# A gate by seven products of quarters, added up in PSUM banks, in a hybrid trunk on one core

## The chip, the core and the metric

The kernel runs on one core of a Trainium2 chip. A core has TensorE (PE; its weight loads are listed apart as PEld), VectorE (DVE), ScalarE (ACT), GpSimd (POOL) and SyncE (SP), which here only issues DMA transfers. Working memory is SBUF, 128 partitions wide; matmul sums are made in PSUM, whose banks hold 128 x 512 fp32 values. The metric is device time in microseconds (us) of one execution.

## The reference

One layer of a trunk on x of 512 x 1024 in fp32. A single projection of the normalised input feeds three branches; each branch's result is multiplied by a sigmoid gate of its own, the three are added, and a feed-forward block follows.

```python
u = rmsnorm(x, ln1_g)
proj = u @ w_in
q, k, v, pool_in, z, xbc, dt_raw, gate_pre = jnp.split(proj, split_idx, axis=-1)
y_a = dilated_attention_mixer(q, k, v, rel_bias) @ w_a     # three groups of six heads
y_b = pool_mixer(pool_in, pool_w, pool_scale) @ w_b
y_c = ssd_mixer(z, xbc, dt_raw, ...) @ w_c
gates = jax.nn.sigmoid(gate_pre + b_gate).reshape(b, s, N_BRANCH, D_MODEL)
merged = gates[:, :, 0] * y_a + gates[:, :, 1] * y_b + gates[:, :, 2] * y_c
x = x + merged @ w_o
x = x + conv_ffn(rmsnorm(x, ln2_g), ffn_w_up, ffn_conv_w, ffn_conv_b, ffn_w_down)
return rmsnorm(x, final_g)
```

The change touches three pieces of `u @ w_in`: the 1024 columns of the second gate (`gates[:, :, 1]`), v of attention groups 1 and 2 (384 columns each, "the pair"), and q and k of attention group 1 (384 columns each).

## The kernel before, in words

**Split products.** Every fp32 operand is split into a high and a low part, and a product is three matmuls: high by high, high by low, low by high (`mm3`, L229 to L237). The activations u (`uh`, `ul`, transposed, 8 tiles of 128 features x 512 tokens) are split once; weights are split job by job.

**Jobs.** A job is a slab of weights, at most 128 x 2048 values, and a `body` that multiplies with it. Its raw tile is loaded by SyncE's DMA queue (`fetch`, L183, two buffers `wraw`), ScalarE makes the high part in two halves (`cast`, L196, three buffers `whp`), VectorE makes the low part (`low`/`lows`, L216, two buffers `wlp`), and a job may have a `then`, which is run behind its low part. The main loop takes the jobs in order: ahead of the body of job n it issues the low part of job n+1, puts the cast of job n+2 in a list that is worked off at the `step()` behind the body's matmuls, and fetches job n+3. Side work (attention, the scan, the convolutions' ends) is kept in generators, and each `step()` advances them by one piece.

**Order.** TensorE, ScalarE, VectorE and GpSimd execute in the order in which the program emits (the `ORDERED` set near the end); only DMA issues on SyncE are placed by a scheduler. The order of jobs is written out in `program()`. Around the change it is: pool projection, v of group 0, q/k of group 0, pool output, the branch product with w_b (its result, kept in `MG`, is what the second gate multiplies), gate chunks 0 to 3, the pair, q/k of group 1, attention of group 1 started as side work, gate chunks 4 to 7, the twelve XBC chunks, the scan.

**The gate.** `gate_jobs(1, ...)` are plain jobs of 256 columns: a chunk of 128 features x 512 tokens is 8 x 3 matmuls of 512 columns in a bank named `pa`, then a sigmoid on ScalarE (L1226) and a product with `MG` on VectorE (L1228).

**Products of quarters.** The pair and q/k of group 1 are done already by seven products for eight (`sevens` and `qk_sevens`): the activations are cut into two halves of features by two halves of tokens, the weights into two halves of rows by two halves of columns; seven products of sums of quarters give the four quarters of the result. The products are named one to seven. Sums of activation quarters come from `sums_of` (four rounds of VectorE and ScalarE, put in the branch product's stage before). Sums of weight quarters are made on VectorE by `diff` (L341), one per step from the last one, and cast and split like a raw tile. Before, each product has a fresh bank (`pb` or `pq`, of four), is copied to SBUF by ScalarE (L370, L735) or read by VectorE with additions to the products that came before, and the quarters of the result are emitted from SBUF (L662 for the pair, L745 for q/k).

Tiles of 128 x 512 fp32 come from a pool of `NBIG` = 54 through `T(name)`; the weight quarters that aren't loaded as raw tiles lie in `ypool`.

Of the kernel before, what the change touches and what calls it, by code (L numbers as in the profile page):

```python
# [10 lines left out]
F32 = mybir.dt.float32  # L11
# [5 lines left out]
P = 128  # L17
# [65 lines left out]
def trunk(ctx: ExitStack, tc, out, x, rel_bias, ln1_g, w_in, b_gate, w_a, pool_w, pool_scale, w_b,  # L83
# [10 lines left out]
    rows = ctx.enter_context(tc.tile_pool(name="rows", bufs=1))  # L94
# [5 lines left out]
    ypool = ctx.enter_context(tc.tile_pool(name="ypool", bufs=2))  # L100
# [221 lines left out]
    def sums_of(f0, f1, ah, al, found):  # L322


        sa, sb = T("sa"), T("sb")
        dve.tensor_tensor(sa[:, LO], f0[:, HI], f1[:, HI], OP.add)
        dve.tensor_tensor(sa[:, HI], sa[:, LO], f0[:, LO], OP.subtract)
        dve.tensor_tensor(sb[:, LO], f0[:, LO], f0[:, HI], OP.subtract)
        dve.tensor_tensor(sb[:, HI], f1[:, LO], sa[:, HI], OP.subtract)
# [13 lines left out]

    def sevens(quarter, c, side, W, emit):

        r1, r2, r3, r5 = {}, {}, {}, {}

        def job(j, load, form, use):  # L350
            def body(ws):
                wh, wl = ws
                parts = side(j)
                for i in range(2):
                    ps = MM("pb")
                    o = slice(i * P, (i + 1) * P)
                    mm3(ps[:, :c], lambda k: wh[:, k, :], lambda k: wl[:, k, :],
                        lambda k: parts[k][0][:, o], lambda k: parts[k][1][:, o], range(4), flip=True)
                    use(i, ps[:, :c])
                step()  # L360
            new = Job([load] if load is not None else [], 4, c, body)
            new.form = form
            if load is None:
                new.load = lambda: None
            return new

        def keep(r, name):
            def use(i, ps):
                r[i] = T(name)[:, :c]
                act.copy(r[i], ps)  # L370
            return use

        def p5(i, ps):
            keep(r5, "r5")(i, ps)
            dve.tensor_tensor(r2[i], r2[i], ps, OP.add)

        def p6(i, ps):
            dve.tensor_tensor(r1[i], r1[i], ps, OP.add)
            emit(0, 1, i, r1[i], r2[i])

        def p7(i, ps):
            r3[i] = T("r3")[:, :c]
            dve.tensor_tensor(r3[i], r1[i], ps, OP.add)
            emit(1, 1, i, r3[i], r5[i])

        one = job("A11", quarter(0, 0), None, keep(r1, "r1"))
        two = job("A12", quarter(1, 0), None, lambda i, ps: emit(0, 0, i, r1[i], ps))
        three = job(4, None, lambda: W[1], keep(r2, "r2"))
        one.then = lambda: diff(one.raw, W[0], one.raw)
        three.then = lambda: diff(W[0], W[1], W[0])  # L390
        two.then = lambda: diff(W[1], W[1], one.raw)
        yield one
        yield three
        yield two
        yield job(1, None, lambda: one.raw, p5)
        yield job(2, None, lambda: W[1], p6)
        yield job(3, None, lambda: W[0], p7)
        yield job("A22", None, lambda: diff(two.raw, two.raw, W[1]),
                  lambda i, ps: emit(1, 0, i, r3[i], ps))
# [3 lines left out]
    def sums_of_u(p):  # L403

        f = []
        for k in (2 * p, 2 * p + 1):
            f.append(T("uf"))
            dve.tensor_tensor(f[-1], uh[:, k, :].bitcast(F32), ul[:, k, :].bitcast(F32), OP.add)
        yield
        yield from sums_of(*f, T("sah", F32R), T("sal", F32R),  # L410
                           lambda j, h, l: US.__setitem__((j, p), (h, l)))
# [32 lines left out]
    def grow(src):  # L444
        g = rows.tile([P, D], F32, name="grow", tag="grow")
        sp.dma_start(g, src.partition_broadcast(P))
        return g
# [11 lines left out]
    def norm_early(t, g):  # L459
# [4 lines left out]
        pool.tensor_tensor(xg, t, g[:, :S], OP.mult)  # L464
# [3 lines left out]
    def norm_late(t, g, v0, outs, last=None):  # L468
# [6 lines left out]
        dve.tensor_tensor(xg, t, g[:, S:], OP.mult)  # L475
# [171 lines left out]
    def v_pair():  # L647

        c, W = C_V + 384, []
        vd = dram.tile([S, 384], F32, name="vdram")  # L650
        rows_ = lambda c0: w_in[:, c0:c0 + 384].rearrange("(k two p) c -> two p k c", two=2, p=P)
        quarter = lambda two, h: rows_(c + 384 * h)[two]

        def load():
            for two in range(2):
                W.append(ypool.tile([P, 4, S], F32, name="w3", tag="xs")[:, :, :384])
                sp.dma_start(W[two], quarter(two, 1))

        def emit(hi, right, i, a, ps):
            g, tb = 1 + right, 2 * hi + i  # L660
            t = T(f"v{g}")
            dve.tensor_tensor(t[:, :384], a, ps, OP.add)  # L662
            if g == 2:
                sp.dma_start(vd[tb * P:(tb + 1) * P, :], t[:, :384])
                return

            for n in range(4):
                if (g, n) not in V:
                    V[g, n] = T(f"vr{g}")
                sp.dma_start(V[g, n][32 * tb:32 * tb + 32, :384], t[n:P:4, :384])  # L670
# [8 lines left out]
        return load, sevens(quarter, 384, side_u, W, emit), residues  # L679
# [20 lines left out]
    def qk_sevens(g):  # L700


        W = []
# [3 lines left out]
        r1, r2, r3, r5 = {}, {}, {}, {}  # L707

        def load():
            for two in range(2):  # L710
                W.append(ypool.tile([P, 4, S], F32, name="w3", tag="xs")[:, :, :384])
                sp.dma_start(W[two], quarter(two, 1))

# [1072 lines left out]
```

## Time and profile before

| | us |
|---|---|
| runs (3) | 1023.88 to 1024.09, median 1024.09 |
| profiled execution | 1024.13 |
| its span | 1022.4 |
| TensorE busy | 1013.1 (99%), 5258 matmuls |
| TensorE weight loads | 857.6 (84%) |
| VectorE busy | 701.4 (69%), 890 instructions |
| ScalarE busy | 507.9 (50%), 847 instructions |
| GpSimd busy | 127.2 (12%), 108 instructions |
| DMA | 118.08 MB, 115 GB/s on average |

The span is the time from the first to the last recorded instruction; the execution's own time has 1.7 us more around it. A line such as `L216 DVE TENSOR_TENSOR wl<-raw,wh 128x2048 ... | 192.5, 2438 | 39.1 <-ACT wh L196` reads: line 216 of the kernel, VectorE, the output and inputs by name, the shape, then the group's busy time in us, the mean of one instruction in ns, and the time that the engine sat idle before these instructions with what ended it. Rows of the timeline begin with the start in us and the duration in us. Rows that begin with a stretch in us (180.50:204.61) give the busy time and the count of instructions of each engine in that stretch, then the clock that was granted to TensorE, the DMA engines' share and GB/s.

### The profile page before, as it was taken

The page shows a single profiled execution, that of the slowest core. Times are in us where ns is not written, and L with a number is a line of the kernel's source. Part 1 is how long each engine was busy: PE and PEld are TensorE (multiplying, and loading weights), DVE is VectorE, ACT ScalarE, POOL GpSimd, SP SyncE. Part 2 cuts the span into 40 slices and gives each one's busy share as a digit, 9 for nine tenths or more (in the row PEclk, how much of TensorE's full clock was granted, in tenths as well). Part 3 has the DMA queues.
Part 4 walks back from the last instruction along what each step waited for, and adds up shares of the span by engine and source line. Part 5 has one row for each costly group of instructions (what it writes and reads, how often), then busy time and mean ns, then how long its engine had stood idle before and what let it go on. Part 6 is the DMA issues. An engine that isn't in the chain of part 4 may idle for free.

```text
span 1022.4 us, 13249 instructions
## 1 busy us (share of the span) xinstructions
PE 1013.1 (99%) x5258; PEld 857.6 (84%) x5258; DVE 701.4 (69%) x890; ACT 507.9 (50%) x847; POOL 127.2 (12%) x108
## 2 busy tenths in 40 slices
PE   8999999999999999999999999999999999999997
PEld 8998878899888888888888888898888888888886
DVE  6563566788766656676879666768778768685756
ACT  5432545454574366878567224554444434433434
POOL 1770000000000000000044501102111100111002
PEclk9999999999999999999999999999999999999999
DMA  8444312124442354552254526542232333321322
GB/s 269 138 118 135 105 62 76 31 83 145 124 118 83 87 151 112 145 138 74 79 140 160 165 83 237 178 142 86 94 113 83 99 107 122 126 83 42 124 83 82
DMA packets 114077, 118.08 MB, mean 115 GB/s; under 512 B 6212, under 2 KB 97927, under 8 KB 114016
## 3 DMA queue, kind: packets, MB, share of 16 engines
q1 hardware_dynamic: 113423, 116.39, 37.0%
q8 instruction: 41, 0.67, 0.3%
q10 hardware_dynamic: 592, 0.86, 0.3%
q14 instruction: 21, 0.16, 0.1%
HBM read 113.44 MB, written 3.00 MB: 114 GB/s over the span
## 4 chain that ended last, share of the span: by engine, by line
PE 98%; DMA 1%; DVE 0%; ACT 0%; ACTq 0%; issue 0%
PE pa L237 36%; PE pu L237 22%; PE pb L237 12%; PE pd L237 7%; PE pqk L237 6%; PE pq L237 3%; PE pa L1633 2%; PE ps L799 1%; PE pu L1434 1%; PE ppw L237 1%; PE po L847 1%; PE pt L833 1%; PE py L1132 1%; DMA xin<-in_x_dram 1%; PE pyo L1139 1%; PE pst L1120 0%
## 5 line engine op out<-in xcount | busy, mean ns | idle before, releaser
L216 DVE TENSOR_TENSOR wl<-raw,wh 128x2048 fp32r<-128x2048 f32 (+3 forms) x95 | 220.1, 2318 | 47.5 <-ACT wh L196 39.7
L196 ACT CAST wh<-raw 128x1024 fp32r<-128x1024 f32 (+4 forms) x187 | 186.5, 1017 | 42.7 <-DVE raw L341 18.0
L1329 DVE SCALAR_TENSOR_TENSOR hc<-pu,fcol,hc 128x510 f32<-128x510 f32 x88 | 65.9, 748 | 56.4 <-ACT hc L1326 54.8
L237 PE MATMUL pa<-uh,wh 128*128 128x512 f32 x384 | 97.0, 395 | 0.0
L237 PE MATMUL pa<-ul,wh 128*128 128x512 f32 x384 | 94.9, 389 | 0.0
L237 PE MATMUL pa<-uh,wl 128*128 128x512 f32 x384 | 94.8, 389 | 0.0
L237 PEld LDWEIGHTS pa<-ul,wh 128*128 128x128 f32 x384 | 72.1, 188 | 15.1
L237 PEld LDWEIGHTS pa<-uh,wl 128*128 128x128 f32 x384 | 72.1, 188 | 14.9
L237 PE MATMUL pu<-uh,wh 128*128 128x512 f32 (+1 forms) x352 | 83.5, 379 | 0.0
L237 PE MATMUL pu<-uh,wl 128*128 128x512 f32 (+1 forms) x352 | 83.5, 379 | 0.0
L237 PE MATMUL pu<-ul,wh 128*128 128x512 f32 (+1 forms) x352 | 83.5, 379 | 0.0
L237 PEld LDWEIGHTS pa<-uh,wh 128*128 128x128 f32 x384 | 70.6, 188 | 14.3
L237 PEld LDWEIGHTS pu<-uh,wl 128*128 128x128 f32 x352 | 64.2, 188 | 12.5
L237 PEld LDWEIGHTS pu<-ul,wh 128*128 128x128 f32 x352 | 64.2, 188 | 12.4
L237 PEld LDWEIGHTS pu<-uh,wh 128*128 128x128 f32 x352 | 64.1, 188 | 12.4
L1326 ACT ACTIVATE hc<-pu,fcol,fcol 128x512 f32<-128x512 f32 x40 | 31.2, 779 | 78.9 <-PE pu L237 78.9
L1334 POOL TENSOR_TENSOR hc<-hc 128x512 f32<-128x512 f32 x22 | 30.8, 1401 | 289.0 <-DVE hc L1329 252.0
L1115 POOL TENSOR_TENSOR st<-st,dts 128x512 f32<-128x512 f32 x4 | 4.5, 1126 | 380.4 <-ACT st L1123 322.0
L821 ACT ACTIVATE sb<-sb,nmls 128x128 f32<-128x128 f32 (+1 forms) x72 | 30.0, 418 | 25.7 <-DVE nmls L818 13.6
L1331 ACT ACTIVATE hc<-hc 128x512 f32<-128x512 f32 x22 | 13.9, 632 | 39.9 <-DVE hc L1329 39.9
L1226 ACT ACTIVATE sg<-pa,col 128x512 f32<-128x512 f32 x24 | 16.5, 689 | 32.1 <-PE pa L237 31.0
L969 DVE SCALAR_TENSOR_TENSOR xs<-pa,col,xs 128x509 f32<-128x509 f32 (+2 forms) x24 | 18.0, 749 | 17.1 <-ACT xs L965 16.6
(393 smaller groups left out, 1872.6 us busy)
## 6 DMA issues: line engine op xcount, KB each, us to landing
raw<-in_w_in_dram SPq DMA_DIRECT2D x25, 1024.0 KB, 5.2
raw<-in_ffn_w_up_dram SPq DMA_DIRECT2D x22, 1024.0 KB, 5.1
raw<-in_w_o_dram SPq DMA_DIRECT2D x8, 1024.0 KB
raw<-in_ffn_w_down_dram SPq DMA_DIRECT2D x8, 1024.0 KB, 5.1
raw<-in_w_in_dram SPq DMA_DIRECT2D x14, 512.0 KB, 4.8
raw<-in_w_in_dram SPq DMA_DIRECT2D x6, 768.0 KB, 4.6
raw<-in_w_b_dram SPq DMA_DIRECT2D x4, 1024.0 KB, 5.1
al<-ad SPq DMA_DIRECT2D x16, 256.0 KB, 7.3
```

The source lines that it names most:

```text
L196: (other.tensor_copy if other and i else act.copy)(job.high[:, :, o], job.raw[:, :, o])
L216: (eng or dve).tensor_tensor(l[:, :, o], job.raw[:, :, o], h[:, :, o].bitcast(F32), OP.subtract)
L237: pe.matmul(ps, l, r, start=first and n == 0, stop=last and n == total - 1, skip_group_check=onto)
L799: pe.matmul(pss[i][:, o:o + w * P], q[r, n * P:(n + 1) * P], k[r, kb * P:(kb + w) * P], start=True, stop=True)
L821: act.activation(sb[:, off:off + w * P], sb[:, off:off + w * P], AF.Exp, bias=nm[:, n, h:h + 1], accum_out=ls[:, n, h:h + 1])
L969: dve.scalar_tensor_tensor(t[:, sh:], ps[:, :S - sh], col[:, o_cw + 12 * k + m:o_cw + 12 * k + m + 1], t[:, sh:], OP.mult, OP.add)
L1226: act.activation(s, ps, AF.Sigmoid, bias=col[:, o:o + 1])
L1326: act.activation(t, ps, AF.Identity, bias=ff["c1"][:, ff["b"] + m:ff["b"] + m + 1], scale=fw(2, m))
L1329: dve.scalar_tensor_tensor(t[:, sh:], ps[:, :S - sh], fw(k, m), t[:, sh:], OP.mult, OP.add)
L1331: act.activation(t, t, AF.Silu)
L1334: pool.tensor_tensor(a, a, t, OP.mult)
L1633: pe.matmul(first[2 * n + j][:, lo:hi], a[:, k, j * P:(j + 1) * P], b[:, k, lo:hi], start=a is wh and b is uh and k == 0, stop=a is wl and ...
```

## The change

The second gate is now also done by seven products of quarters, and all three groups (gate, pair, q/k) share one class, `Seven`. A group uses two pairs of PSUM banks, A and B. Product two has B to itself and its result is kept in SBUF (`keep`, ScalarE); five opens B and is kept; three adds onto five in the bank and is kept. One opens A; six, seven and four add onto it, one behind the other, and after one, six and seven VectorE adds the bank's sum to a kept product or takes it off (`done`; in place, for q/k straight into their tiles), which makes a quarter of the result; after four the bank holds the last quarter. For the gate ScalarE then takes sigmoids of 128 x 256 pieces (four per product), and the product with `MG` follows a step later (`total(m)`), when a 128 x 512 chunk is whole.

Of the sums of weight quarters one in four is made by four DMA transfers on GpSimd's queue that add a quarter from DRAM onto a loaded tile (`plus`); the other three stay on VectorE (`total`). The groups interlock: the next group's two comes ahead of the last group's four. The sums of activations are spread over two stages and made with other signs (`turned`); attention of group 1 is called behind the gate, pair and q/k groups and one XBC job. `ypool` has three buffers, `NBIG` is 52, and the row of gains is loaded as two T tiles in place of one tile of a pool of its own.

By the emitted order, TensorE has 5402 matmuls for 5258: 192 of 512 columns are replaced by 336 of 256. The pair and q/k keep theirs.

```diff
-    rows = ctx.enter_context(tc.tile_pool(name="rows", bufs=1))
...
-    ypool = ctx.enter_context(tc.tile_pool(name="ypool", bufs=2))
+    ypool = ctx.enter_context(tc.tile_pool(name="ypool", bufs=3))
...
-    def sums_of(f0, f1, ah, al, found):
...
+        plus, minus = (OP.subtract, OP.add) if turned else (OP.add, OP.subtract)
         sa, sb = T("sa"), T("sb")
-        dve.tensor_tensor(sa[:, LO], f0[:, HI], f1[:, HI], OP.add)
...
+    class Seven:
+        def __init__(self, quarter, c, widths, product, done, name):
+            R, A, B, W = {}, [], [], [None, None]
+            def tile_of(i):
+                W[i] = ypool.tile([P, 4, S], F32, name="w3", tag="xs")[:, :, :c]
+                sp.dma_start(W[i], quarter(i, 1))
+            def plus():
+                for k in range(4):
+                    pool.dma_start(W[0][:, k, :], quarter(0, 0)[:, k, :], accum_op=OP.add)
+            def total(out, a, b, op=OP.add):
+                dve.tensor_tensor(out, a, b, op)
+                return out
+            def job(j, raw, form, bank, use, more=False):
+                def body(ws):
+                    if not more:
+                        bank[:] = [MM(name) for _ in range(2)]
+                    for i in range(2):
+                        product(bank[i], ws, side_u(j), i, more)
+                        use(i, bank[i][:, :widths[i]])
+                    step()
+                new = Job([raw] if raw is not None else [], 4, c, body)
+                new.form = form
+                if raw is None:
+                    new.load = lambda: None
+                return new
+            def keep(hi, right):
+                def use(i, ps):
+                    r = R[hi, right, i] = T("r7")[:, :widths[i]]
+                    act.copy(r, ps)
+                return use
+            def end(hi, right, op=None):
+                return lambda i, ps: done(hi, right, i, R.get((hi, right, i)), ps, op)
+            self.two = job("A12", quarter(1, 0), None, B, keep(0, 0))
+            five = job(1, None, lambda: W[0], B, keep(1, 1))
+            three = job(4, None, lambda: W[1], B, keep(0, 1), True)
+            one = job("A11", quarter(0, 0), None, A, end(0, 0, OP.add))
+            six = job(2, None, lambda: W[0], A, end(0, 1, OP.subtract), True)
+            seven = job(3, None, lambda: W[1], A, end(1, 1, OP.subtract), True)
+            four = self.four = job("A22", quarter(1, 0), lambda: total(four.raw, four.raw, W[0]), A,
+                                   end(1, 0), True)
+            five.then = lambda: total(W[0], W[0], W[1])
+            one.then = lambda: total(W[1], W[0], one.raw, OP.subtract)
+            self.jobs = five, three, one, six, seven
+            self.load = lambda: tile_of(0), plus, lambda: tile_of(1)
...
+        def product(ps, ws, parts, i, more):
+            o = slice(i * P, (i + 1) * P)
+            mm3(ps[:, :384], lambda k: ws[0][:, k, :], lambda k: ws[1][:, k, :],
+                lambda k: parts[k][0][:, o], lambda k: parts[k][1][:, o], range(4), flip=True, onto=more)
+        def done(hi, right, i, r, ps, op):
             g, tb = 1 + right, 2 * hi + i
-            t = T(f"v{g}")
-            dve.tensor_tensor(t[:, :384], a, ps, OP.add)
+            if r is None:
+                r = T(f"v{g}")[:, :384]
+                act.copy(r, ps)
+            else:
+                dve.tensor_tensor(r, r, ps, op)
...
+    def by_features(chunks):
+        def product(ps, ws, parts, i, more):
+            for n, m in enumerate(chunks[i]):
+                o = slice(m * P, (m + 1) * P)
+                mm3(ps[:, 256 * n:256 * n + 256], lambda k: ws[0][:, k, o], lambda k: ws[1][:, k, o],
+                    lambda k: parts[k][0], lambda k: parts[k][1], range(4), onto=more or n > 0)
+        return product
...
+        def done(hi, right, i, r, ps, op):
+            which = "qk"[right]
...
+                view = (plain if right else grouped)(QK[which, g, m], g)[:, :, 64 * hi:64 * hi + 64]
...
+                if r is None:
+                    dve.tensor_copy(view, piece(ps))
+                else:
+                    dve.tensor_tensor(view, piece(r), piece(ps), op)
...
+    def gate_seven(b):
+        quarter = lambda two, h: w_in[:, C_GATE + b * D + S * h:C_GATE + b * D + S * h + S].rearrange(
+            "(k two p) c -> two p k c", two=2, p=P)[two]
+        chunks = ((0, 1), (2, 3))
+        def total(m):
+            dve.tensor_tensor(MG[m], MG[m], SG[b, m], OP.mult)
             return
...
+        def done(hi, right, i, r, ps, op):
+            if r is not None:
+                dve.tensor_tensor(r, r, ps, op)
+            for n, m in enumerate(chunks[i]):
+                m += 4 * right
+                if (b, m) not in SG:
+                    SG[b, m] = T("sg")
+                o = o_bg + 8 * b + m
+                act.activation(SG[b, m][:, 256 * hi:256 * hi + 256],
+                               (ps if r is None else r)[:, 256 * n:256 * n + 256],
+                               AF.Sigmoid, bias=col[:, o:o + 1])
+                if hi:
+                    running.append(after(1, total(m)))
+        return Seven(quarter, S, (512, 512), by_features(chunks), done, "pa")
...
         yield from v_jobs(0)
+        yield Call(lambda: running.extend(after(3 * p, sums_of_u(p)) for p in (0, 1)))
         yield from qk_jobs(0)
         yield from pool_out_job()
         yield Call(lambda: attend(0))
         yield Call(lambda: waiting.insert(3, ssd_prep()))
+        gates = gate_seven(1)
+        pair, residues_of_v = v_pair()
+        groups = gates, pair, qk_sevens(1)
         for i, job in enumerate(branch_jobs(1, w_b, YB, 8, more=range(7))):
-            if i == 3:
-                yield Call(lambda: running.extend(after(p, sums_of_u(p)) for p in range(4)))
+            if i == 1:
+                yield Call(gates.load[0])
+            if i == 2:
+                yield Call(lambda: running.extend(after(2 * p - 4, sums_of_u(p)) for p in (2, 3)))
+                yield Call(gates.load[1])
+                yield Call(gates.load[2])
             yield job
-        load, pair, residues_of_v = v_pair()
-        yield Call(load)
-        yield from gate_jobs(1, 0, SPLIT)
-        loads, qk = qk_sevens(1)
-        for i, job in enumerate(pair):
-            yield job
-            if i == 4:
-                yield Call(loads)
-        yield from qk
+        last = None
+        for group, next_ in zip(groups, groups[1:] + (None,)):
+            yield group.two
+            if last:
+                yield last.four
+            last = group
+            for i, job in enumerate(group.jobs):
+                if next_ and i >= 2:
+                    yield Call(next_.load[i - 2])
+                yield job
+        xbc = jobs_a(w_in, C_XBC, 12, uhk, ulk, KD, xbc_evac)
+        yield next(xbc)
+        yield last.four
         yield Call(lambda: attend(1))
         yield Call(lambda: running.extend(after(2, f()) for f in (residues_of_v, residues_of_bias)))
-        yield from gate_jobs(1, SPLIT)
-        yield from jobs_a(w_in, C_XBC, 12, uhk, ulk, KD, xbc_evac)
+        yield from xbc
...
-NBIG = 54
+NBIG = 52
```

More of the change, by code (lines that the diff above doesn't have):

```diff
@@ L342, in diff @@
         return out
[L344 to L399, printed above, removed]
@@ L474, in norm_late @@
         xg = T("xg")
-        dve.tensor_tensor(xg, t, g[:, S:], OP.mult)
+        dve.tensor_tensor(xg, t, g[1], OP.mult)
         if last:
```

84 lines of the change are left out of this document (15 added, 69 removed).

## The prediction

> **What bounds the kernel.** I read the page's slices and chain first, then the chain of waits on TensorE, then the busy times by stage.
>
> ```profile
> span 1022.4 us, 13249 instructions
> PE   8999999999999999999999999999999999999997
> DVE  6563566788766656676879666768778768685756
> PEclk9999999999999999999999999999999999999999
> PE 98%; DMA 1%; DVE 0%; ACT 0%; ACTq 0%; issue 0%
> ```
> ```profile
> PE uT L1650 <- DVE diag L1662: 1.4, 2, 0.8
> PE pa L1592 <- DVE ones L1583: 1.1, 1, 1.1
> ```
> ```profile
> 180.50:204.61 24.11, 24.11 (x131) 19.86 (x130) 16.80 (x25) 11.09 (x18) 0.00 (x0) 1.00 0.11 33
> 204.61:233.76 29.15, 29.15 (x170) 29.14 (x168) 24.38 (x25) 13.39 (x21) 0.00 (x0) 1.00 0.38 115
> 233.76:263.99 30.23, 30.23 (x254) 30.23 (x254) 26.25 (x28) 13.62 (x20) 0.00 (x0) 1.00 0.34 110
> 263.99:293.00 29.01, 29.01 (x155) 23.68 (x154) 17.71 (x23) 22.78 (x42) 0.00 (x0) 1.00 0.44 133
> ```
> TensorE is the whole chain, and its only waits lie in the first 10 us. The last rows are the changed stretch: gate chunks 0 to 3, the pair, the q/k sevens, then gate chunks 4 to 7 (columns: sum, PE, PEld, DVE, ACT, POOL, clock). TensorE is busy throughout at full clock, so the time here is TensorE's work plus any wait that the change creates. VectorE is the next engine: 24.38 of 29.15 and 26.25 of 30.23 us where products of quarters run now, 16.80 of 24.11 where the gate runs. The profiled execution took 1024.13 us, its span and 1.7 around it; the median of the runs is 1024.09, so the sum needs no shift.
>
> **TensorE's work.**
> ```profile
> 328.58 1.98 PE L237 MATMUL pa<-uh,wh 128*128 128x512 f32 x8
> 330.40 1.98 PE L237 MATMUL pa<-ul,wh 128*128 128x512 f32 x8
> ```
> ```profile
> 240.94 0.64 PE L237 MATMUL pq<-sbh,wh 128*128 128x256 f32 x4
> 241.43 0.64 PE L237 MATMUL pq<-sbl,wh 128*128 128x256 f32 x4
> ```
> Starts give the pitch: 8 of 512 columns in 1.82 us, 0.227 each. The q/k stage has 7 x 36 = 252 matmuls of 256 columns in 30.23 us, 0.120 each (0.49 per 4 in the last rows). The gate had 8 chunks x 24 = 192 matmuls of 512 columns, 43.5 us; it gets 7 products x 48 = 336 of 256 columns, 40.3 us. Gain: 3.2 us. An eighth of 43.5 would be 5.4; the half-width shape gives 2.2 of it back, since in the q/k stage the weight loads are as busy as the matmuls (30.23 of 30.23). The pair (168 matmuls in 29.15 us, 0.1735 each, 4.16 per product) and q/k (4.32 per product) keep their counts and shapes.
>
> **What the banks cost.** Before, every product took a fresh bank of four. Now one, six, seven and four add onto the same two banks, and each product's sum must be read out before the next may write. So product i+1 waits for: VectorE's read of bank 0 after product i, and its own low half (wl). VectorE and ScalarE go in program order: within a product VectorE does the next product's low, then the reads of two banks; ScalarE does four sigmoids, then the cast of the product after next. These durations go in:
>
> ```profile
> 268.07 2.28 DVE L216 TENSOR_TENSOR wl<-raw,wh 128x2048 fp32r<-128x2048 f32 x1
> ```
> ```profile
> 237.10 1.75 DVE L216 TENSOR_TENSOR wl<-w,wh 128x1536 fp32r<-128x1536 f32 x1
> 238.77 1.75 DVE L341 TENSOR_TENSOR w<-w,w 128x1536 f32<-128x1536 f32 x1
> ```
> ```profile
> 265.32 2.00 ACT L196 CAST wh<-raw 128x1024 fp32r<-128x1024 f32 x2 [5.24 <-DMA raw<-in_w_in_dram]
> ```
> ```profile
> 238.53 1.57 ACT L196 CAST wh<-raw 128x768 fp32r<-128x768 f32 x2
> 241.15 0.59 ACT L735 COPY rq<-pq 128x512 f32<-128x512 f32 x1 [1.04 <-PE pq L237]
> ```
> ```profile
> L341 DVE TENSOR_TENSOR raw<-w,raw 128x2048 f32<-128x2048 f32 x2 | 4.6, 2280 | 0.0
> L1484 DVE TENSOR_TENSOR x<-x,pb 128x512 f32<-128x512 f32 x8 | 5.4, 684 | 2.1 <-PE pb L237 2.1
> L1226 ACT ACTIVATE sg<-pa,col 128x512 f32<-128x512 f32 x24 | 16.5, 689 | 32.1 <-PE pa L237 31.0
> L821 ACT ACTIVATE sb<-sb,nmls 128x256 f32<-128x256 f32 x18 | 9.1, 504 | 19.2 <-DVE nmls L810 12.0 <-DVE nmls L818 7.1
> ```
> ```profile
> 204.61 0.87 PE L237 MATMUL pb<-wh,uh 128*128 128x384 f32 x4
> 204.81 0.69 ACT L1226 ACTIVATE sg<-pa,col 128x512 f32<-128x512 f32 x1 [2.98 <-PE pa L237]
> 205.54 0.69 DVE L1228 TENSOR_TENSOR yo<-yo,sg 128x512 f32<-128x512 f32 x1 [2.25 <-ACT sg L1226]
> ```
> A bank's reader starts 0.2 us after its last matmul (204.61 to 204.81); ScalarE to VectorE takes 0.04. A sigmoid of 256 columns has no row: between the 128x256 exponential's 0.504 and zero its pitch, back to back, I take as 0.42 (the 512 sigmoid's 0.689 less the 0.3 by which a 256 one is shorter); the ends of 0.35 and 0.50 move each step's four by 0.3 either way.
>
> With t from the start of the gate's product one:
> - A product's cast is issued behind the readers of the product two before it: ScalarE copies three's second bank (0.2 to 0.8), then casts six by 2.7; VectorE has low six at 5.05, reads one's first bank by 5.66. Six may start at 5.76: no wait.
> - One's second bank is done at 5.76, read by 6.65; sigmoids to 7.5; cast seven to 9.5; low seven to 11.8; only then VectorE reads six's first bank, to 12.43. Seven starts at 12.5 where 11.52 was due: 1.0 lost.
> - Six's second bank is read by 13.0; sigmoids to 14.1; cast of the pair's first product to 15.65, its low to 17.4; four's combination (2.28) to 19.6; VectorE reads seven's two banks to 20.8; sigmoids to 21.8; cast four to 22.85 (first half) and 23.8; low four to 26.1. TensorE is through seven at 18.3 and the pair's first product at 22.4, waits 0.4 for the first half, does 8 of four's 48 matmuls, and waits 2.3 for the low half. 2.75 lost.
>
> Against 27.2 of plain work four ends near 31: a loss of 3.7, all because low four sits behind ScalarE's sigmoids. The same working for the pair: low six comes at 4.5 (a 1.57 cast, a 1.75 low, the reads) where the product takes 4.16: 0.35. For q/k six waits for two reads of 0.6 behind its low, 4.99 against 4.32: 0.65. Bounds of these three together: 1.0 at least (only seven's wait, if the second stretch overlaps one handover more), 7 at most (below).
>
> **What is moved or free.** The bank restarts after waits: a pipeline break costs 0.1 (1.98 for eight against 1.82), twice or three times, 0.2. The remaining edits lie beside other work:
> - Gate chunks 4 to 7 lay beside attention of group 1; their sigmoids alternated with its exponentials, and each change reloads ScalarE's table:
>
> ```profile
> L1226 ACT ACT_TABLE_LOAD x10 | 12.8, 1283 | 0.2
> ```
> Six such loads fall away. TensorE never waited for them, so they are worth zero; uncovered each would be 1.28. Attention then lies beside ten XBC chunks where it had 4 gate and 12 XBC chunks; ScalarE was busy 22.78 of 29.01 us there with sigmoids and loads that are now gone, so it still ends under the chunks.
> - The gate's multiplication by its branch (8 of 0.69) is queued on VectorE behind low four and ahead of the pair's low one; counted in the lows that follow, still inside 4.16 of slack per product.
> - One of four combinations becomes four adding transfers on GpSimd's queue, in three groups. No row shows such a transfer; the nearest are GpSimd's last row ahead of the gate and two loads:
>
> ```profile
> 72.18 0.22 POOL L925 TENSOR_TENSOR psw<-psw,ramp 128x16 f32<-128x16 f32 x1
> ```
> ```profile
> raw<-in_w_in_dram SPq DMA_DIRECT2D x14, 512.0 KB, 4.8
> raw<-in_w_in_dram SPq DMA_DIRECT2D x6, 768.0 KB, 4.6
> ```
> The gate's and the pair's first quarters are now loaded at the head of SyncE's queue (three buffers), so both groups can be added from 72.4 on, as soon as GpSimd is through with that row; five's low wants them near 175. Only the third group waits, for the buffer that the gate gives up at four's combination, and q/k's five comes some 30 us later or more. At twice a load's time, 10 us for each, nothing is late; they cost zero while they take under 25 us, and at 35 the third would cost up to 10. GpSimd does nothing else in all four windows, so nothing is queued behind them that TensorE wants.
> - Behind SyncE's issues stand the raw loads, whose order is the old one; the DMA share is 0.11 to 0.44 in the four windows, so a raw tile keeps its 4.6 to 5 us and has a product's 5.76 after its buffer is free (two buffers: one is loaded while the other is cast). q/k and the pair had this in products of 4.2.
> - The opening moves 0.75 MB more (two tiles of 1.0 MB and one of 0.75 for two of 0.75 and a row of gains of 0.5). In the two rows by fortieth parts of the first 45 us (the DMA's share in tenths, then GB/s) that is 2.1 us at 350 GB/s, of a queue that then has a gap:
>
> ```profile
> DMA  0389999999999712489999999994000005990000
> GB/s 0 38 237 370 293 374 318 293 327 347 357 382 390 202 26 69 38 261 375 386 409 384 332 370 363 349 350 144 1 0 0 0 0 60 333 329 6 0 0 0
> ```
> ```profile
> 32.21 1.91 ACT L196 CAST wh<-raw 128x2048 fp32r<-128x2048 f32 x1
> ```
> The share falls to zero at some 31 us, and the cast that would feel the shift starts at 32.21. Zero, 1 us at the most.
> - Sums of the activations (four steps on VectorE and ScalarE) go in two pairs, one of them into the first q/k stage, where the slices of VectorE show 5 to 7 tenths. Zero, or 0.5 if a low slips behind them.
> - Two T tiles fewer (52), the gains' row loaded in two halves ahead of its use instead of at the start: zero, unless a tile is short.
>
> **The sum.** -3.2 + 3.7 + 0.35 + 0.65 + 0.2 = +1.7: 1025.8 us. From the bounds: -3.2 + 1.0 = -2.2 (1021.9), and -3.2 + 7 + 0.5 = +4.3 (1028.4). Of these the value stands nearest the middle because each of its starts is taken from a row, and only the sigmoid's pitch is not.
>
> **Rivals.**
> (1) The waits are hidden. If the reads and sigmoids come 1 us earlier each, by ScalarE taking cast seven ahead of one's last sigmoids or by finer waits on a tile's halves, only four's wait is left. The break-even is a loss of 3.2. For it: VectorE has 5 us spare per 29 now. Against: program order on ScalarE and the working above, which leaves no room. With a loss of 1.0: 1021.9. This ends on the other side.
> (2) More waits than counted. Here waits are held until a whole tile is written (a cast's second half, 23.8 for 22.85, adds 0.95 to four and as much to seven), and the pair's group takes the shift on, each product of it with 0.35. That is 2 x 0.95 + 4 x 0.35 = 3.3 more: 1029.
> (3) A late adding transfer: one group 5 us late gives 1030.8. The rows for loads speak against it.
> (4) The clock falls after a wait. The profile shows full clock everywhere with waits of at most 1.1 us; a wait of 2.3 is outside what it shows. The product behind four's wait (40 matmuls, 4.8 us) would run longer, by nothing at the least and by twice at the most: in the middle +2.4, 1028.2. The Trainium skill, "TensorE: Matmul & The Clock Gate", section "What's actually happening", says that the clock halves after an idle window of some 3.4 us, and returns after as much work; by that rule the wait here would be too short. If it did bite, its estimate is half of 3.4 us lost, 1.7.
>
> **Chances.** The forecast's case 0.50 (its own range 1024.5 to 1027.3), 1 0.22, 2 0.18, 3 0.05, 4 0.05. A measurement of this kernel tells 0.2% (2.05 us) from no change: under 1022.04 is faster, above 1026.14 slower. Faster holds most of rival 1: 0.17. Within 0.2% the rest of it and half of the forecast's case: 0.35. Slower: the other half, 2, 3 and 4, 0.48. The range goes from 1021.6 (rival 1) to 1029.5 (rival 2), leaving out late transfers and the deeper gains.
>
> **What would show it.** Waits of TensorE, none before in this stretch: on VectorE's read of six (pa) for 1.0 and on low four (wl) for 2 to 2.5; smaller ones in pb and pq. Gate matmuls of 256 columns at 0.120. The adding transfers all ended 15 us ahead of their products. Wrong it is if TensorE shows no wait on wl in gate four (rival 1), or waits on the tile that the adding transfer writes (rival 3), or a clock below 1.00 (rival 4).

## The result

The changed kernel takes 1029.3 us (median of 6, 1028.06 to 1029.51) where the kernel before takes 1024.0 (median of 6): a ratio of 1.0048, 95% interval 1.0035 to 1.0061. It is slower by 5.3 us, near the top of the range and 3.5 us above the point forecast. In a later batch the same kernel gave 1029.34 (median of 5, 1027.92 to 1030.68) beside 1024.05. Its executions fall into two groups: 4 of 11 lie at 1027.9 to 1028.3, 7 at 1029.2 to 1030.7. The profiled execution took 1028.16 us, span 1025.6, and belongs to the lower group.

From the page after the change, the span, the busy times and the chain:

```profile
span 1025.6 us, 13613 instructions
...
PE 1010.9 (99%) x5402; PEld 861.3 (84%) x5402; DVE 707.7 (69%) x886; ACT 511.2 (50%) x863; POOL 136.7 (13%) x120
...
PE 95%; DVE 2%; ACT 2%; DMA 1%; issue 0%; ACTq 0%
```

TensorE is busy for 1010.9 us where it was 1013.1, and yet the span is 3.2 us longer: VectorE and ScalarE now have 2% each of the chain, where they had none. TensorE's waits say where:

```profile
PE uT L1641 <- DVE diag L1653: 2.1, 2, 1.6
PE pa L236 <- DVE wl L215: 2.1, 1, 2.1
PE pa L1583 <- DVE ones L1574: 1.1, 1, 1.1
PE po L827 <- ACT sb L814: 0.8, 1, 0.8
PE pa L236 <- DVE r L741: 0.7, 1, 0.7
PE pq L236 <- DVE q L725: 0.6, 1, 0.6
PE pb L236 <- ACT wh L195: 0.2, 1, 0.2
PE pa L236 <- ACT wh L195: 0.2, 1, 0.2
```

The first and third are the opening's, where the first real product (uT) starts at 6.99 us in both kernels; the `uT` wait is 0.7 us longer only because the 24 warming matmuls ahead of it were through 0.8 us earlier in this execution. The other six are new. Here they are on TensorE's timeline (start, duration, and in brackets the idle time and what ended it):

```profile
167.50 0.87 PE L827 MATMUL po<-sb,v 128*64 128x128 f32 x10 [0.82 <-ACT sb L814]
...
213.79 0.71 PE L236 MATMUL pa<-sbh,wh 128*128 128x256 f32 x4 [0.69 <-DVE r L741]
...
224.17 0.74 PE L236 MATMUL pa<-uh,wh 128*128 128x256 f32 x4 [0.22 <-ACT wh L195]
224.75 0.64 PE L236 MATMUL pa<-ul,wh 128*128 128x256 f32 x4
227.45 0.74 PE L236 MATMUL pa<-uh,wl 128*128 128x256 f32 x4 [2.07 <-DVE wl L215]
...
245.22 0.93 PE L236 MATMUL pb<-wh,sah 128*128 128x384 f32 x4 [0.22 <-ACT wh L195]
...
275.76 0.71 PE L236 MATMUL pq<-sah,wh 128*128 128x256 f32 x4 [0.57 <-DVE q L725]
```

The second row is the gate's seven, the next three its four, then six of the pair and six of q/k. Measured from where the product before would have ended, they cost 0.84, 0.38, 2.22, 0.39 and 0.73, with two small ones of 0.11 and 0.07 together 4.74 us; the forecast had 3.7 + 0.35 + 0.65 = 4.7. Breaks at these places and at changes of shape cost another 0.5 (behind a wait the first group of four takes up to 0.58 to the next start, 224.17 to 224.75, in place of 0.48). The gate's 336 matmuls of 256 columns run at 0.120, as forecast: 182.24 to 187.03 has ten groups of four, 0.479 each. The first row is another matter: it lies in the branch stage, and shifts all that follows by 1.24 us. So the span: -3.2 + 4.74 + 0.5 + 1.24 = +3.3, where +3.2 was measured.

The largest wait, on four's low half, comes about as follows on VectorE and ScalarE (in order of time):

```profile
218.56 2.29 DVE L359 TENSOR_TENSOR raw<-raw,w 128x2048 f32<-128x2048 f32 x1
220.76 1.27 DVE L741 TENSOR_TENSOR r<-r,pa 128x512 f32<-128x512 f32 x2
221.47 1.71 ACT L747 ACTIVATE sg<-r,col 128x256 f32<-128x256 f32 x4 [4.62 <-DVE r L741]
223.09 1.98 ACT L195 CAST wh<-raw 128x1024 fp32r<-128x1024 f32 x2
225.10 2.29 DVE L215 TENSOR_TENSOR wl<-raw,wh 128x2048 fp32r<-128x2048 f32 x1 [3.07 <-ACT wh L195]
```

Four's combination is ready at 220.85. ScalarE has been idle for 4.62 us by the time VectorE has read seven's first bank, but in program order the four sigmoids come first; so the cast starts at 223.09, the low half at 225.10, and TensorE goes on at 227.45.

For six of the pair the row names ScalarE's cast. The cast whose first half ends there (244.38 to 245.17) is of a later product, though; six's own cast and its low half were through by 244.6. What is left is VectorE's read of the bank, which stands behind that low half and ends for the first bank at 245.07:

```profile
242.85 1.76 DVE L215 TENSOR_TENSOR wl<-w,wh 128x1536 fp32r<-128x1536 f32 x1 [0.47 <-ACT wh L195]
244.52 1.06 DVE L661 TENSOR_TENSOR r<-r,pb 128x384 f32<-128x384 f32 x2
```

Two things lie outside this trace: the time around the span grew from 1.7 us to between 2.1 and 2.6, and in most executions 1.2 us or more come on top.

### The profile page after: what moved, and what is told of

The parts are those of the page before. It is cut to its first block, busy times and chain, and to the rows that moved or that the text cites. A ratio compares the mean times of both kernels' runs of the same rounds, so it can differ in the third digit from the quotient of the medians.

```text
span 1025.6 us, 13613 instructions
## 1 busy us (share of the span) xinstructions
PE 1010.9 (99%) x5402; PEld 861.3 (84%) x5402; DVE 707.7 (69%) x886; ACT 511.2 (50%) x863; POOL 136.7 (13%) x120
## 4 chain that ended last, share of the span: by engine, by line
PE 95%; DVE 2%; ACT 2%; DMA 1%; issue 0%; ACTq 0%
PE pa L236 34%; PE pu L236 22%; PE pb L236 12%; PE pd L236 7%; PE pqk L236 6%; PE pq L236 3%; PE pa L1624 2%; PE ps L779 1%; PE pu L1414 1%; PE po L827 1%; PE ppw L236 1%; ACT wh L195 1%; DVE wl L215 1%; PE pt L813 1%; PE py L1112 1%; DMA xin<-in_x_dram 1%
## 5 line engine op out<-in xcount | busy, mean ns | idle before, releaser
L215 DVE TENSOR_TENSOR wl<-raw,wh 128x2048 fp32r<-128x2048 f32 (+3 forms) x92 | 214.1, 2328 | 60.6 <-ACT wh L195 52.7
L195 ACT CAST wh<-raw 128x1024 fp32r<-128x1024 f32 (+4 forms) x181 | 181.3, 1021 | 53.8 <-DVE raw L359 15.9
L236 PE MATMUL pa<-uh,wh 128*128 128x512 f32 (+1 forms) x368 | 88.9, 381 | 0.2 <-ACT wh L195 0.2
L236 PE MATMUL pa<-uh,wl 128*128 128x512 f32 (+1 forms) x368 | 86.9, 375 | 2.1 <-DVE wl L215 2.1
L236 PE MATMUL pa<-ul,wh 128*128 128x512 f32 (+1 forms) x368 | 86.8, 375 | 0.0
L236 PEld LDWEIGHTS pa<-uh,wl 128*128 128x128 f32 x368 | 66.7, 188 | 14.7 <-DVE wl L215 2.3
L236 PEld LDWEIGHTS pa<-ul,wh 128*128 128x128 f32 x368 | 66.7, 188 | 12.6
L236 PEld LDWEIGHTS pa<-uh,wh 128*128 128x128 f32 x368 | 65.3, 188 | 12.4 <-ACT wh L195 0.5
L215 DVE TENSOR_TENSOR wl<-w,wh 128x2048 fp32r<-128x2048 f32 (+1 forms) x18 | 38.0, 2111 | 12.4 <-ACT wh L195 7.8
L195 ACT CAST wh<-w 128x1024 fp32r<-128x1024 f32 (+1 forms) x36 | 32.8, 954 | 2.4 <-DVE w L341 2.4
## 6 DMA issues: line engine op xcount, KB each, us to landing
raw<-in_w_in_dram SPq DMA_DIRECT2D x24, 1024.0 KB, 6.1
raw<-in_ffn_w_up_dram SPq DMA_DIRECT2D x22, 1024.0 KB, 5.2
raw<-in_w_o_dram SPq DMA_DIRECT2D x8, 1024.0 KB, 5.3
raw<-in_ffn_w_down_dram SPq DMA_DIRECT2D x8, 1024.0 KB, 5.1
raw<-in_w_b_dram SPq DMA_DIRECT2D x4, 1024.0 KB, 5.2
w<-in_ffn_w_down_dram SPq DMA_DIRECT2D x4, 1024.0 KB, 5.0
```

The lines of the kernel that those rows point to most:

```text
L195: (other.tensor_copy if other and i else act.copy)(job.high[:, :, o], job.raw[:, :, o])
L215: (eng or dve).tensor_tensor(l[:, :, o], job.raw[:, :, o], h[:, :, o].bitcast(F32), OP.subtract)
L236: pe.matmul(ps, l, r, start=first and n == 0, stop=last and n == total - 1, skip_group_check=onto)
```

## The experiments

**The changed kernel once more.**

> The changed kernel as it is. Its six executions so far fell into two groups, 1028.1 (spans 1025.6 and 1026.0) and 1029.2 to 1029.5 (spans 1026.8 to 1027.1, a granted clock lower by 0.001). Theory: the second group comes from TensorE's clock falling for a short time behind the 2.1 us wait in the gate's last product, in some executions; then both groups appear again, about one execution in three in the lower one, and a trace of the upper group shows a clock below 1.00 within some us behind that wait. Rival: the groups have to do with the end or the start of the program, and a trace of the upper group shows the extra 1.2 us elsewhere, with the clock at 1.00 in the changed stretch.

Measured: 1028.26, 1030.04, 1029.34, 1027.92, 1030.68 us; granted clock 0.998 for the two at 1028, 0.995 to 0.997 for the others. Both groups are there again. The execution that was profiled was once more one of the lower group, with the same six waits and a clock of 1.00, so this run leaves the theory open. Traces of three other runs below settle it.

**The gate's sigmoids one step later.**

```diff
+            def sigmoids():
                 for n, m in enumerate(chunks[i]):
...
+            if r is None:
+                for _ in sigmoids():
+                    pass
+            else:
+                running.append(after(1, sigmoids()))
```

> The gate's sigmoids behind products one, six and seven are issued one step later, so that ScalarE takes the next casts first; nothing else differs. Theory of the prediction's chain (the sigmoids hold back the casts of seven and four, and with them the lows): the waits of TensorE ahead of seven (0.84 in the trace), ahead of four (0.38) and on four's low half (2.22) go, with their restarts 3.7 us in all; the time falls from 1029.3 to 1025.6, and the pair's and q/k's waits (0.4 and 0.7) stay. Rival (VectorE's own order of low halves, combinations and reads is what is late): the wait on four's low half stays over 1.5 and the time falls by less than 1.5 us. If the upper group of executions comes from the long wait, it is gone here as well and the runs lie within 0.5 us of each other.

Measured: 1026.18 us (median of 11; ten of them 1025.7 to 1026.6, one 1027.46 at a clock of 0.996), 3.1 us less. They do not all lie within the 0.5 us that was expected. The gate's waits are gone, all three. Two new ones stand in the pair:

```profile
239.60 0.96 PE L236 MATMUL pb<-wl,uh 128*128 128x384 f32 x4 [0.95 <-DVE wl L215]
243.49 0.94 PE L236 MATMUL pb<-wh,sah 128*128 128x384 f32 x4 [0.85 <-DVE r L661]
```

VectorE's timeline of this run shows why:

```profile
231.30 1.76 DVE L215 TENSOR_TENSOR wl<-w,wh 128x1536 fp32r<-128x1536 f32 x1 [1.04 <-ACT wh L195]
232.97 4.90 DVE L735 TENSOR_TENSOR yo<-yo,sg 128x512 f32<-128x512 f32 x8
237.79 1.75 DVE L215 TENSOR_TENSOR wl<-raw,wh 128x1536 fp32r<-128x1536 f32 x1
```

With the sigmoids the gate's eight multiplications fell into one step: 4.9 us of VectorE ahead of the low half of the pair's product one. The theory's mechanism holds (ScalarE's sigmoids held back the casts, the casts the lows): the pair's five starts 3.6 us sooner (228.77 for 232.34), as the 3.7 of the theory has it. That the sum of 1025.6 came so close is in part luck. Of these 3.6 the pair gives back 1.8 by its new waits (its six starts at 243.49 for 245.22), which the sum missed; and it missed that the median would leave the upper group of executions, and that the time around the span would be 2.1 for 2.4.

**The second pair of sums later.**

```diff
-                yield Call(lambda: running.extend(after(2 * p - 4, sums_of_u(p)) for p in (2, 3)))
+                yield Call(lambda: running.extend(after(p + 1, sums_of_u(p)) for p in (2, 3)))
```

> The second pair of sums of activations starts three and two steps later in the branch stage; nothing else differs. Theory: TensorE's wait of 0.82 us in attention of group 0 (1.24 us of shift in all), which the kernel before does not have, comes from these sums, whose tiles or work stand in the way of that attention's copies; it goes, and the time falls by 1.2, to 1028.1. Rival (the wait has another cause, such as the adding transfers on the queue or the fewer tiles alone): it stays, and the time with it. The gate's waits are as before the edit in both cases, unless the sums now come late for product five, which would show as a wait ahead of it.

Measured: 1027.89 us (median of 5): one at 1026.3, four at 1027.75 to 1028.4, where the changed kernel's groups are at 1027.9 to 1028.3 and at 1029.2 to 1030.7. In the same batch each group is 1.8 to 2.0 lower; 1.3 to 1.6 of that is span, where 1.2 was expected, and 0.4 lies around it. The wait of 0.82 is gone:

```profile
165.18 1.75 PE L827 MATMUL po<-sb,v 128*64 128x128 f32 x28
166.86 0.92 PE L779 MATMUL ps<-k,q 64*128 64x256 f32 x8
```

Here the profiled execution is one of the upper group, and it shows what that is. The same stretch behind four's wait, first in windows of 2 us (the third number from the end is the granted clock), then on TensorE:

```profile
224.00:226.00 2.00, 0.02 (x1) 0.00 (x0) 2.00 (x2) 1.92 (x4) 0.02 (x1) 0.98 0.03 12
226.00:228.00 2.00, 1.91 (x9) 1.91 (x10) 2.00 (x5) 0.00 (x0) 2.00 (x3) 0.50 0.42 40
228.00:230.00 2.00, 2.00 (x14) 2.00 (x14) 2.00 (x2) 0.28 (x1) 0.63 (x1) 0.67 0.93 318
230.00:232.00 2.00, 2.00 (x19) 2.00 (x18) 1.87 (x2) 0.56 (x2) 0.00 (x0) 1.00 1.13 204
```
```profile
226.09 1.22 PE L236 MATMUL pa<-uh,wl 128*128 128x256 f32 x4 [2.07 <-DVE wl L215]
227.11 1.05 PE L236 MATMUL pa<-uh,wh 128*128 128x256 f32 x4
227.96 1.05 PE L236 MATMUL pa<-ul,wh 128*128 128x256 f32 x4
228.82 0.87 PE L236 MATMUL pa<-uh,wl 128*128 128x256 f32 x4
229.52 0.64 PE L236 MATMUL pa<-uh,wh 128*128 128x256 f32 x4
...
232.40 0.86 PE L236 MATMUL pb<-wh,sah 128*128 128x384 f32 x4
```

Behind the wait of 2.07 us the clock is at 0.50; groups of four take 0.85 to 1.02 us to the next start in place of 0.48, until about 229.3. From the restart to the next product it takes 6.31 us, where the changed kernel's profiled execution takes 4.89 (227.45 to 232.34): 1.42 us lost.

**Without the adding transfers.**

```diff
-            self.load = lambda: tile_of(0), plus, lambda: tile_of(1)
+            self.load = lambda: tile_of(0), lambda: None, lambda: tile_of(1)
```

> The twelve adding transfers on GpSimd's queue are left out, so one term is missing from a combination of weights in each of the three groups, and the output is not the reference's; all other work is there. Theory: the transfers are hidden (the span stays within 0.3 us), but the queue that they need costs time outside the span: it was 1.7 us around the span before and is 2.1 to 2.6 us now, so the time falls by 0.4 to 0.9. Rival (the transfers delay something): the span itself gets shorter by 0.5 us or more. Second rival: neither changes, and the larger rest around the span has another cause.

Measured: 1029.07 us (median of 5, 1027.32 to 1029.6). The spans are those of the changed kernel (1025.5 for the one of the lower group, 1027.1 to 1027.8), with the same six waits: the transfers delay nothing. Around the span are 1.77 to 1.83 us, where the changed kernel has 2.44 to 2.58 in the same batch and the kernel before 1.7 to 1.8. The median is only 0.3 under that of the changed kernel in the same batch because four of five executions are of the upper group here and three of five there; group by group it is 0.8. The theory holds by this run; the one with a plain gate, below, takes some of that back. The profiled execution again has a lower clock behind the 2.06 us wait (0.58 and 0.56 in the windows 228 to 230 and 230 to 232), and 6.40 us from the restart to the next product, 1.51 lost.

**Both edits, and the multiplications spread.**

```diff
-                        running.append(after(1, total(m)))
+                        running.append(after(LATER[m], total(m)))
...
+LATER = (1, 2, 6, 6, 0, 0, 1, 1)
```

> The gate's sigmoids one step later and the sums three and two steps later, both as in the runs before, and the gate's eight multiplications by its branch spread over the steps of the pair's products instead of eight at once (they stood as 4.9 us of VectorE ahead of the low half of the pair's product one). Theory: every wait of TensorE but those in the pair's and q/k's product six is the queue of ScalarE or VectorE ahead of a low half; then the waits of 0.95 and 0.85 in the pair fall to about 0.4, the one of 0.82 in attention is gone, and the time is 1026.2 - 1.6 - 1.2 = 1023.4, with all executions within 0.6 us of each other, since no wait is left that the clock could fall behind. Rival (VectorE has too much work in this stretch whatever the order): waits of 1.5 us or more turn up elsewhere in the pair or q/k, and the time stays above 1025.

Measured: 1023.08 us (median of 11, 1022.82 to 1023.75), a ratio of 0.9989 (0.998 to 0.9998) to the kernel before. Beside the opening's two, TensorE has two waits left:

```profile
PE pq L236 <- DVE q L725: 0.6, 1, 0.6
PE pb L236 <- ACT wh L195: 0.2, 1, 0.2
```

All eleven executions lie within 0.9 us (0.6 was expected) at a clock of 0.998 or 0.999: without the long wait there is no upper group here.

**More tiles.**

```diff
-    ypool = ctx.enter_context(tc.tile_pool(name="ypool", bufs=3))
+    ypool = ctx.enter_context(tc.tile_pool(name="ypool", bufs=2))
...
-NBIG = 52
+NBIG = 56
```

> The changed kernel with 56 tiles of 128 x 512 in place of 52, paid for with two buffers for the loaded quarters in place of three; the sums stay where the change put them. Only the wait in attention of group 0 is to be read. Theory: that wait is a shortage of tiles (a tile asked for by ScalarE's and VectorE's next instruction is still held for matmuls that come later on TensorE), so with four more it is gone. Rival: it is the work of the sums on VectorE and ScalarE, and stays at 0.8 us. With two buffers the loads of the later groups may come later, and waits there can be longer than in the changed kernel.

Measured: the wait is gone, with the sums where the change put them. ScalarE in the changed kernel, then in this one:

```profile
162.66 0.61 ACT L333 CAST sbh<-sb 128x512 fp32r<-128x512 f32 x1
166.50 0.59 ACT L1018 ACTIVATE east<-pact 16x512 f32<-16x512 f32 x1 [3.23 <-PE po L827]
167.00 0.45 ACT L814 COPY sb<-pt 128x384 f32<-128x384 f32 x1
```
```profile
162.66 0.62 ACT L333 CAST sbh<-sb 128x512 fp32r<-128x512 f32 x1
163.19 0.58 ACT L1018 ACTIVATE east<-pact 16x512 f32<-16x512 f32 x1
163.67 0.45 ACT L814 COPY sb<-pt 128x384 f32<-128x384 f32 x1
```

`east` reads nothing of `po`; in the changed kernel it waits 3.23 us for a tile that the attention's first `po` matmuls still read, and the copy of `sb` behind it is what the last ten of these matmuls need. The work of the sums is the same in both. So it is a shortage of tiles, and moving the sums by some steps cures it as well as four more tiles do. Whether the two tiles taken away or the earlier sums would make it alone, no run separates.

As a whole this kernel took 1037.92 us in its one execution. With two buffers q/k's quarter is loaded late (issued at 248.79), the last adding transfer onto it is issued at 261.99, ScalarE's cast of the tile waits for it until 268.30, and TensorE waits 6.7 us. So an adding transfer that comes late does cost what rival 3 feared; in the changed kernel none did. Behind the gate's 2.07 us wait this execution, too, has the clock at 0.50, and 6.38 us from the restart to the next product, 1.49 lost.

**The gate in plain chunks again.**

```diff
-        groups = gates, pair, qk_sevens(1)
+        groups = pair, qk_sevens(1)
...
+        yield from gate_jobs(1)
```

> The second gate is computed by eight plain chunks of 512 columns again, ahead of the pair; the pair and q/k keep the sums in banks, the adding transfers and everything else of the change. Theory: the parts of the time are separate, so this has TensorE's 3.2 us of work back, has none of the gate's waits, and keeps the pair's and q/k's (0.4 and 0.7 with restarts), the attention's 1.24 and 0.3 to 0.7 outside the span: 1024.05 + 2.6 to 3.1 = 1026.6 to 1027.1. Rival: the pair's and q/k's waits were only the gate's backlog on ScalarE and VectorE and are gone without it: 1025.7 to 1026.1.

Measured: 1026.98 us (median of 9, 1026.85 to 1027.52), ratio 1.0026 (1.0016 to 1.0036). The waits are those of the pair's and q/k's six (0.3 and 0.6) and attention's 0.8: they don't hang on the gate. Around the span are 1.72 to 1.79 us, though eight of the twelve adding transfers are still there.

**The next low half between the two reads.**

```diff
                         use(i, bank[i][:, :widths[i]])
+                        if new.late and i == 0:
+                            new.prepare()
...
+            one.late = six.late = True
...
-        chunks = ((0, 1), (2,))
+        chunks = ((0,), (1, 2))
...
-        return Seven(quarter, 384, (512, 256), by_features(chunks), done, "pq")
+        return Seven(quarter, 384, (256, 512), by_features(chunks), done, "pq")
...
```

> The kernel with the spread multiplications, and in products one and six the next low half is issued between the reads of the two banks instead of ahead of both; for q/k the bank with one chunk comes first. Theory: the remaining waits (0.4 at the pair's six, 0.6 at q/k's) are a read that stands behind the low half on VectorE, and go; the time is 1.0 to 1.2 under the kernel with the spread multiplications alone, 1022.2 by its forecast. Rival: the low half is now what is late, and TensorE waits for it after 8 matmuls of six for about as long; the time is the same.

Measured: 1021.64 us (median of 8, 1021.35 to 1022.04), ratio 0.9974 (0.9964 to 0.9984) to the kernel before, 1.4 under the kernel with the spread multiplications (0.3 of it around the span) and 7.7 under the change as it was made. TensorE has no wait left beyond the opening's:

```profile
PE uT L1654 <- DVE diag L1666: 1.7, 2, 1.0
PE pa L1596 <- DVE ones L1587: 1.1, 1, 1.1
```

VectorE in the gate's products shows the new order, read, low half, read:

```profile
203.35 0.69 DVE L744 TENSOR_TENSOR r<-r,pa 128x512 f32<-128x512 f32 x1 [1.64 <-PE pa L236]
203.96 2.28 DVE L215 TENSOR_TENSOR wl<-w,wh 128x2048 fp32r<-128x2048 f32 x1
206.23 0.69 DVE L744 TENSOR_TENSOR r<-r,pa 128x512 f32<-128x512 f32 x1
```

Six of the pair starts at 240.03 here, while the cast of a later product that its row named before is still in its first half (from 239.57): it was the read that it had waited for. The gain over the kernel before, 2.6 us in its batch (1024.23), is TensorE's 3.2 less 0.2 that is still outside the span and some breaks. It is the change with every wait taken out of it, and the fastest of all these kernels.

## Why the prediction came out as it did

- **TensorE's gain, 3.2 us: right.** 256-column matmuls at 0.120, and with the gate plain the gain is gone: that kernel is 2.75 us slower than the kernel before in its batch, which is the other waits (0.39, 0.73 and 1.24) and some 0.4 of breaks, with no gain to set against them.
- **The chain through the gate, 1.0 for seven and 2.75 for four: right in place, cause and size** (0.84, and 0.38 + 2.22). Putting the sigmoids behind the casts removes all three waits, so it is ScalarE's order that costs them.
- **Six of the pair 0.35, six of q/k 0.65: right** (0.39, 0.73). They stay when the gate is plain, and go when the low half no longer stands ahead of both reads.
- **The restarts, 0.2: too small**; breaks and changes of shape cost 0.5.
- **"Two T tiles fewer (52) [...] zero, unless a tile is short", and the sums "Zero, or 0.5": here the working failed.** A tile was short, in the branch stage, and cost 1.24. I had priced the sums by the engines' busy shares and never counted live tiles; with 56 tiles and the same work of the engines it is gone.
- **The clock, given 1 in 20: it falls in 7 of 11 executions**, and takes 1.4 to 1.5 us. The rival's middle price was 2.4, and the estimate that the prediction worked out from the Trainium skill 1.7. I gave it so little because the wait was shorter than the idle time that the page names; the wait came out close to the forecast, 2.07 for 2.3 us, and was long enough. By the prediction's own sign, a clock below 1.00, rival 4 is what these seven executions show, on top of the forecast's waits.
- **The time around the span, taken as 1.7: it grew by 0.4 to 0.9.** No term of the sum stood for it. Without the adding transfers it is back; but with eight of the twelve it is back too, and with all twelve it is 1.9 to 2.6 in different kernels. What sets it stays open.
- **Rival 1 (hidden waits), 1021.9:** not this kernel, but the order that it named, casts ahead of sigmoids, is what the first edit does, and the last kernel shows that the waits can be hidden. Rival 2 (waits held to a whole tile): no; four starts on the first half of its cast. Rival 3: no; the last adding transfer is issued by 231 us and q/k's cast of that tile starts at 258.39.

Of the 5.3 us, then, 2.0 are the mechanism that was worked out (forecast 1.7), and the rest came from three places priced at nothing or as a side case: tiles 1.24, the time outside the span 0.7 by the middle of the runs, and the clock, which takes the median into the upper group, 1.2 to 1.5.

That 1029.3 still lies inside the range, up to 1029.5, is luck: this end came from rival 2, which did not happen, and the forecast's own range ended at 1027.3, below even the lower group of executions. The chances are also added up wrongly: half of the forecast's 0.50 with rivals 2, 3 and 4 makes 0.53 for slower and leaves 0.30 for within 0.2%, where the prediction has 0.48 and 0.35.

## What to carry to other kernels

Where a bank is added to by products one behind the other, write down each engine's queue between two of them, in program order; a queue longer than the product is a wait, and moving work that nobody waits for (here sigmoids, then multiplications) behind the cast removes it, if the moved work does not land in one lump ahead of the next low half. When tiles are taken away and work is moved earlier, count the tiles that are alive at that place, not only the engines' busy shares. A saving of TensorE's work that leaves a wait of two microseconds can cost more than the wait, because the clock may fall behind it (here 1.4 to 1.5 us on top of 2.07).

## What the hardware showed that was not expected

A wait of 2.06 to 2.07 us, behind 0.96 us of work and a wait of 0.2, is enough for the granted clock to fall to 0.50 in some executions (7 of 11 of the changed kernel by their times; the traces of three other runs with the same wait show it), and not in others with the same waits to within 0.1 us.

Read in windows of 0.02 us, the clock is at 0.50 from 225.92 to 229.34 in the run with the later sums, from 228.34 to 231.75 in the run without the adding transfers, and from 227.38 to 230.79 in the run with 56 tiles. That is 3.41 us each time, but it begins 0.17 us ahead of TensorE's restart in the first, 0.18 behind it in the second and 1.18 behind it in the third. In the run with 56 tiles the clock falls once more at 264.93, in the wait of 6.7 us, and is back at 275.18: from one of its four changes to the next it is 1, 10 and 3 times 3.41 us. So in this trace the clock changes on steps of 3.41 us that run on through 48 us of work and waits, and not at a fixed time behind a wait. In the step that ended with the fall TensorE had been idle for 2.14, 2.06 and 2.07 us in the three runs, some 60% of it.

The Trainium skill, "TensorE: Matmul & The Clock Gate", section "What's actually happening", states that the clock halves after at least one idle window of some 3.4 us and is back after as long a busy one, and that the window runs freely. The depth (0.50), the length (3.41 us) and the free running agree with it; the idle time needed does not, if the whole window has to be idle: 2.1 us of it did. That an execution keeps its clock when a step ends in the middle of the wait would fit, but is not shown: the two traced executions of the changed kernel have no change of the clock there by which their steps could be placed. What the least idle time is stays open, too. One execution of eleven with waits of 0.95 and 0.85 us, 4 us apart, was 1.3 us longer at a clock of 0.996; it was not traced, and whether such short waits do it too stays open.
